# Hybrid encoder trunk on one core: one weight split moved from POOL to VectorE, and four squares and three head-pair splits moved to POOL

## The chip, the cores and the metric

The kernel runs on one core of a Trainium2 chip. The metric is the time of one execution on the device in microseconds (us). Several executions of the kernel before gave a median of 967.95 us. The engines are called as the profile calls them: PE is TensorE (its matmuls; PEld its weight loads), DVE is VectorE, ACT is ScalarE, POOL is GpSimd, SP issues the DMAs, and PSUM is the memory into which PE writes its results.

## The reference

The input is 512 frames of 1024 channels in fp32. Two layers follow each other; each is a mixer and a feed-forward block, both with an RMS norm ahead and a residual sum behind. The first layer's mixer pools over trailing windows, the second's is chunked attention with 16 heads of 64 channels. The change lies in and just ahead of the attention, which is this:

```python
qkv = h @ w_qkv                              # h: the normed input
q, k, v = jnp.split(qkv, 3, axis=-1)
q = head_rmsnorm(q.reshape(B, S, N_HEADS, HEAD_DIM), q_norm)
k = head_rmsnorm(k.reshape(B, S, N_HEADS, HEAD_DIM), k_norm)
...
s = jnp.einsum('bqhd,bkhd->bhqk', qc, kb).astype(jnp.float32) * scale + bias[None]
s = jnp.where(valid[None, None, None, :], s, -1e30)
p = jax.nn.softmax(s, axis=-1).astype(vb.dtype)
return jnp.einsum('bhqk,bkhd->bqhd', p, vb)  # then joined and multiplied by w_o
```

`head_rmsnorm` divides each head's 64 numbers by the root of their mean square: these are the squares that the change speaks of.

## The kernel before

**Split products.** Every fp32 product is made from parts. A matrix is split into a rounded part `hi` and the rest `lo` (`split`, L97 to L103: `hi` is a copy, on ACT unless another engine is named; `lo` is a subtraction, on DVE unless another is named), and PE makes three products, hi·hi, hi·lo and lo·hi, which it sums in PSUM (`mm3`, L121). Weights come by DMA and are split once they land (`load_split`, L110).

**Stages.** The first layer fills the span up to about 335 us. From there `opening` (a list of steps written by hand, with the order of PE, DVE, ACT and SP as written) makes the values, the norm's statistics and the first projection. The attention loop runs from about 440 us, and the second feed-forward block closes the program.

**The attention loop.** Work is a list of 64 tiles, 16 heads by four blocks of 128 frames. At each tile PE gets, in this order: `scores` of that tile (L1394 and L1395; DVE adds the bias and takes the minimum at L1398, ACT makes the exponentials at L1400 and scales by the reciprocal sums at L1402, all in tiles `sb`), at two places in each head pair `channel_major` (four transposes `zt` at L1364 that bring a projected pair into channel order, then ACT and DVE at L107, L108, L1368 and L1371 split it and POOL copies a half at L1375), `turn` of the tile two places back (transposes `tp` at L1410 of the scaled tile `sb`, split at L102 and L103 into `pt0` or `pt1`), and `mix` of the head whose last tile is four places back (`oo` at L1422; ACT copies half of it into `ob` at L1427 and DVE adds it into the pair's output `o` at L1428). Between these steps `fill` pulls matmuls from a list of fillers in proportion to the loop's progress: `second` (the second projection, begun in `opening`), `project(2)`, `project(3)` and then the output products `wo`.

**A projection.** `project(c)` makes queries and keys of heads 4c to 4c+3, that is of two head pairs. `products` (L1279) takes four slices of the weights `wqk`, each with two column halves: the matmuls `qk` at L123 to L125. `hi` of a slice is made by ACT, `lo` by POOL, since `project` hands `nc.gpsimd` as `eng` (L1314). For the second projection the first slice is `ready`: `opening` has loaded and split it (L1261 and L1262, `lo` on DVE). When a frame block t is done, `evict(t)` copies it into `Z[c, t]` (the tiles `z`; even t by ACT at L1310, odd t by DVE at L1308), and `squares(t)` is put off to the next step of the loop: ACT squares it into `zs` (L1300), DVE sums each head's 64 squares (L1301). Behind the four of them comes `norms` (L1315): two small operations on DVE (`qk_a`), a logarithm and an exponential on ACT (L135, L136, `qk_t` and `qk_y`), four more on DVE (L137 to L139, L1319), and then four multiplications of the tiles `z` by `qk_y` on POOL (L1321). The transposes `zt` of the pair need those four tiles.

**Splits of head pairs.** When the last head of a pair is mixed, the pair's output `O2[kept]` is split for the output products into `XS[kept]` and `XS[KD + kept]` (L1482): two halves of the tiles that the profile calls `two`, `hi` by ACT and `lo` by DVE. The weights `wo` of the output products for pairs one to six are split by POOL (`wo_h` at L100, `wo_l` at L103).

**What sets the order.** In the attention loop PE's order is that of the code. The orders of ACT, DVE, POOL and SP are set by the scheduler of the framework, from its own estimates of when each operation can run, and are then fixed in the program: each engine runs its list from front to back and waits at an operation whose input isn't there.

Of the kernel before, what the change touches and what calls it, by code (L numbers as in the profile page):

```python
# [19 lines left out]
AF = mybir.ActivationFunctionType  # L20
# [6 lines left out]
KD = D // P  # L27
# [45 lines left out]
def trunk(ctx: ExitStack, tc: tile.TileContext, xt, xT, cols, band, edge, poolw, gv, wout, wqk, wv, wo, rel, out):  # L73
    nc = tc.nc
# [14 lines left out]
    def psum(tag, name, bufs=2):  # L89
        return ps.tile([P, S], F32, name=name, tag=tag, bufs=bufs)  # L90
# [3 lines left out]
    def g_tile(name):  # L94
        return tmp.tile([P, S], F32, name=name, tag="g", bufs=6)

    def split(raw, hi, lo, eng=None, eng_hi=None):  # L97

        if eng_hi:
            eng_hi.tensor_copy(hi, raw)  # L100
        else:
            nc.scalar.activation(hi, raw, AF.Copy)  # L102
        return (eng or nc.vector).tensor_sub(lo, raw, hi.bitcast(F32))  # L103
# [6 lines left out]
    def load_split(src, n, name, pool=None, eng=None, tag=(None, None), eng_hi=None):  # L110

        raw = wp.tile([P, 1024], F32, name=f"{name}_r", tag="wr")
        if pool:
            hi, lo = (pool.tile([P, n], F32R, name=f"{name}_{c}", tag=t, bufs=2 if t == "as" else 1) for c, t in zip("hl", tag))
        else:
            hi, lo = (wp.tile([P, 1024], F32R, name=f"{name}_{c}", tag=f"w{c}", bufs=2) for c in "hl")
        nc.sync.dma_start(raw[:, :n] if len(src.shape) == 2 else raw.rearrange("p (a b) -> p a b", a=src.shape[1]), src)
        split(raw[:, :n], hi[:, :n], lo[:, :n], eng, eng_hi)
        return hi, lo

    def mm3(o, sh, sl, mh, ml, first, last, **how):  # L121

        yield nc.tensor.matmul(o, sh, mh, start=first, stop=False, **how)  # L123
        yield nc.tensor.matmul(o, sh, ml, start=False, stop=False, **how)  # L124
        yield nc.tensor.matmul(o, sl, mh, start=False, stop=last, **how)  # L125

    def run(steps):
        step = None
        for step in steps:
            pass  # L130
        return step

    def rsqrt(a, y, t):

        nc.scalar.activation(t, a, AF.Ln)  # L135
        seed = nc.scalar.activation(y, t, AF.Exp, scale=-0.5)  # L136
        nc.vector.scalar_tensor_tensor(t, y, -0.5, y, op0=OP.mult, op1=OP.mult)  # L137
        nc.vector.tensor_mul(t, t, a)
        return seed, nc.vector.scalar_tensor_tensor(y, t, 1.5, y, op0=OP.add, op1=OP.mult)  # L139
# [775 lines left out]
    def attention(rest, hook, hidden_slots):  # L915
        XS = set2
        O2, V, Z, QK, SM = {}, {}, {}, {}, {}
# [6 lines left out]
        def norms_of(c):  # L924
            return [big.tile([P, 8 * TT], F32, name=f"qk{c}_{v}", tag="nw", bufs=4) for v in "sayt"]

        def by_frame(v):
            return v.rearrange("p (t h) -> p t h", t=TT)
# [350 lines left out]
        def products(ov, w, name, eng=None, evict=None, ready=None):  # L1279

            for kk in range(4):
                hi, lo = ready if ready and kk == 0 else load_split(w[kk], 1024, f"{name}_{kk}", eng=eng)

                for c, t in [(c, t) for c in range(2) for t in range(TT)] if kk < 3 else [(c, t) for t in range(TT) for c in range(2)]:
                    k = 2 * kk + c
                    s = slice(c * S, (c + 1) * S)
                    q = slice(t * P, (t + 1) * P)
                    yield from mm3(ov[t], XS[k][:, q], XS[KD + k][:, q], hi[:, s], lo[:, s], k == 0, k == KD - 1)
                    if kk == 3 and c and evict:
                        evict(t)  # L1290

        def project(c, banks="PQ", ready=None):

            ov = [psum(banks[t // 2], f"qk{c}_{t}", BANKS[banks]) for t in range(TT)]
            ss, a, y, t_ = norms_of(c)
            s3, a3, y3 = (by_frame(v) for v in (ss, a, y))

            def squares(t):
                sq = g_tile(f"zs{c}_{t}")
                nc.scalar.activation(sq, Z[c, t].rearrange("p h d -> p (h d)"), AF.Square)  # L1300
                nc.vector.tensor_reduce(s3[:, t, :], sq.rearrange("p (h d) -> p h d", d=HD), axis=mybir.AxisListType.X, op=OP.add)  # L1301


            def evict(t):
                Z[c, t] = z = zp.tile([P, 8, HD], F32, name=f"z{c}_{t}", tag="z", bufs=8)
                flat = z.rearrange("p h d -> p (h d)")
                if t % 2:
                    nc.vector.tensor_copy(flat, ov[t])  # L1308
                else:
                    nc.scalar.activation(flat, ov[t], AF.Copy)  # L1310
                late.append(lambda: squares(t))

            yield from products(ov, wqk[c], f"wqk{c}", nc.gpsimd, evict, ready)

            def norms():  # L1315
                nc.vector.tensor_mul(a3, s3, r2[:, :, None].to_broadcast([P, TT, 8]))
                nc.vector.tensor_scalar(a, a, EPS, None, op0=OP.add)
                rsqrt(a, y, t_)
                nc.vector.tensor_mul(y3, y3, rcol[:, :, None].to_broadcast([P, TT, 8]))  # L1319
                for t in range(TT):  # L1320
                    nc.gpsimd.tensor_mul(Z[c, t], Z[c, t], y3[:, t, :, None].to_broadcast([P, 8, HD]))  # L1321

            late.append(norms)
# [34 lines left out]
        def channel_major(p, i):  # L1358


            zt = psum("S", f"zt{p}_{i}", 4)
            for t in range(TT):
                j = 4 * i + 2 * (p % 2)
                nc.tensor.transpose(zt[:, t * P:(t + 1) * P], Z[p // 2, t][:, j:j + 2, :].rearrange("p h d -> p (h d)"), ident)  # L1364
            zh, z2 = (big.tile([P, S], F32R, name=f"z{c}{p}_{i}", tag="zqk", bufs=8) for c in "h2")
            zl = None if i else g_tile(f"zl{p}_{i}")
            if i:
                nc.scalar.activation(zh, zt, AF.Copy, scale=gq[:, i:i + 1])  # L1368
                for e in range(2):
                    hs = slice(e * HD, (e + 1) * HD)  # L1370
                    nc.vector.scalar_tensor_tensor(KL[p % 2][e][hs], zt[hs], gq[hs, i:i + 1], zh[hs].bitcast(F32), op0=OP.mult, op1=OP.subtract)  # L1371
            else:
                split_scaled(zt, gq[:, i:i + 1], zh, zl)

            nc.gpsimd.tensor_copy(z2[HD:], zh[HD:].bitcast(F32))  # L1375
            moves = [(z2[:HD], (z2 if i else zl)[HD:]), (zh[HD:], (zh if i else zl)[:HD])]
            for o, x in moves:
                nc.sync.dma_start(o.bitcast(F32), x if x.dtype == F32 else x.bitcast(F32))
            QK[p, i] = (zh, z2)
# [65 lines left out]
        with tc.manual_schedule(engines={mybir.EngineType.PE}):  # L1445
            cur, done, kept = 0, 0, 0

            def fill(upto):

                nonlocal cur, done  # L1450
                while cur < len(fillers):
                    g, n, a, b = fillers[cur]
                    due = n * (upto - a) / (b - a)
                    while done < min(due, n):
                        next(g)
                        done += 1
                    if upto < b:
                        return
                    run(g)
                    cur, done = cur + 1, 0  # L1460

            fill(0)
            for i in range(nb + LAG + LAGM):
                steps = []
                if i < nb:
                    steps.append(lambda: scores(*tiles_[i]))
                if i % 8 in CM and i // 8 + 1 < NPAIR:
                    steps.append(lambda: channel_major(i // 8 + 1, CM.index(i % 8)))
                j = i - LAG
                if 0 <= j < nb:  # L1470
                    steps.append(lambda: turn(*tiles_[j]))
                j2 = j - LAGM
                if 0 <= j2 < nb and j2 % TT == TT - 1:
                    steps.append(lambda: mix(tiles_[j2][0]))
                for x, step in enumerate(steps):
                    step()
                    if late and x < 2:
                        late.pop(0)()
                    fill(i + (x + 1) / len(steps))

                while 8 * kept + 7 <= j2 and (cur == 3 or cur == 2 and done >= 24 * (kept // 2 + 1)):
                    split(O2[kept], XS[kept], XS[KD + kept])  # L1482
                    kept += 1
            fill(nb + FO)
        assert kept == NPAIR
# [96 lines left out]
```

## Time and profile before

| what | value |
|---|---|
| median of 3 runs | 967.95 us (967.49 to 968.1) |
| the profiled execution | 968.78 us |
| its span, from the first to the last instruction | 967.0 us |
| mean granted clock of TensorE | 1.00 |
| PE busy | 956.6 us (99%), 4958 matmuls |
| DVE busy | 848.4 us (88%) |
| ACT busy | 593.9 us (61%) |
| POOL busy | 94.5 us (10%), 82 instructions |
| DMA, mean over the span | 107 GB/s |

A row of the timeline has the start of an instruction counted from the span's start, its length, its engine, the line of the kernel, the operation, what it writes and reads (numbers left out of the names), the shape, and, where the engine stood idle ahead of it, how long and for whom. Consecutive instructions of a kind can be shown as one row with their count; the length then runs from the first one's start to the last one's end. Matmuls are pipelined: in a full stretch one of 512 columns starts some 0.23 us behind the other, though each is shown as 0.39 or 0.40 us long, so that a stall of PE is read from the distance of starts. The windows view gives the busy time of each engine in a stretch, with the number of instructions.

### The profile page before, as it was taken

What the parts mean: (1) busy time and instruction counts of PE and PEld (TensorE: products, weight loads), DVE (VectorE), ACT (ScalarE), POOL (GpSimd) and SP (SyncE); (2) the same over time, 40 slices, a digit from 0 to 9 for tenths busy, and PEclk for the clock granted to TensorE, in tenths of its full rate; (3) what the DMA queues carried; (4) which work ended last, traced back from release to release, by engine and by line L of the source; (5) the groups of instructions that cost most, each with busy time, mean ns of one, the idle gap of its engine ahead of it and who ended that gap; (6) DMA issues with size and microseconds to landing.
All of it is one profiled execution on the core that took longest, in us unless ns stands there. A gap on an engine that the chain in (4) does not pass through costs nothing.

```text
span 967.0 us, 13737 instructions
## 1 busy us (share of the span) xinstructions
PE 956.6 (99%) x4958; PEld 810.7 (84%) x4958; DVE 848.4 (88%) x1521; ACT 593.9 (61%) x1023; POOL 94.5 (10%) x82
## 2 busy tenths in 40 slices
PE   8999999999999999999999999999999999999998
PEld 7788988888888888888888787888988888888886
DVE  8999999999899859895777887999999999989953
ACT  7665554655555447466898888656565565466531
POOL 2300000000000000044435442000000000000000
PEclk9999999999999999999999999999999999999999
DMA  8222332332323317024443241332233233332323
GB/s 344 70 99 71 115 107 82 120 119 80 113 82 120 101 46 294 22 66 130 126 122 97 87 119 55 100 110 80 93 115 107 84 121 113 100 104 79 115 77 112
DMA packets 38996, 103.87 MB, mean 107 GB/s; under 512 B 4464, under 2 KB 7936, under 8 KB 38928
## 3 DMA queue, kind: packets, MB, share of 16 engines
q1 hardware_dynamic: 38864, 102.95, 32.8%
q8 instruction: 39, 0.64, 0.3%
q14 instruction: 29, 0.24, 0.1%
q0 software_dynamic: 32, 0.04, 0.0%
q10 hardware_dynamic: 32, 0.00, 0.0%
HBM read 96.65 MB, written 2.14 MB: 102 GB/s over the span
## 4 chain that ended last, share of the span: by engine, by line
PE 87%; DVE 9%; ACT 2%; DMA 1%; issue 1%; DVEq 0%; ACTq 0%
PE st_m L593 10%; PE out L124 8%; PE out L125 8%; PE out L123 8%; PE st_m L595 5%; PE st_t L593 5%; PE gv L124 4%; PE gv L123 4%; PE gv L125 4%; PE qk L123 3%; PE qk L124 3%; PE qk L125 3%; PE st_t L595 3%; PE st_b L593 3%; PE tp L1410 2%; DVE one L108 1%
## 5 line engine op out<-in xcount | busy, mean ns | idle before, releaser
L124 PE MATMUL out<-one,ow_h 128*128 128x512 f32 x224 | 88.2, 394 | 0.0
L123 PE MATMUL out<-one,ow_h 128*128 128x512 f32 x224 | 88.0, 393 | 0.0
L125 PE MATMUL out<-one,ow_l 128*128 128x512 f32 x224 | 88.0, 393 | 0.0
L829 DVE TENSOR_TENSOR X<-out,X 128x512 f32<-128x512 f32 (+1 forms) x65 | 44.4, 685 | 46.0 <-PE out L125 45.7
L593 PE MATMUL st_m<-two,g_h 128*128 128x512 f32 x240 | 75.2, 394 | 0.4 <-ACT v L602 0.4
L593 PE MATMUL st_m<-h,g_h 128*128 128x512 f32 x240 | 74.1, 390 | 0.0
L392 ACT ACTIVATE ow_h<-wo_r 128x768 fp32r<-128x768 f32 (+1 forms) x56 | 44.5, 794 | 42.9 <-PE out L124 40.7
L407 DVE SCALAR_TENSOR_TENSOR c<-a,col,c 128x511 f32<-128x511 f32 (+1 forms) x76 | 57.0, 752 | 0.0
L593 PEld LDWEIGHTS st_m<-h,g_h 128*128 128x128 f32 x240 | 45.1, 188 | 10.3
L595 PEld LDWEIGHTS st_m<-two,g_l 128*128 128x128 f32 x240 | 45.1, 188 | 9.6
L593 PEld LDWEIGHTS st_m<-two,g_h 128*128 128x128 f32 x240 | 44.0, 188 | 10.8 <-ACT w L602 0.8
L393 DVE TENSOR_TENSOR ow_l<-wo_r,ow_h 128x768 fp32r<-128x768 f32 (+1 forms) x56 | 50.5, 902 | 2.2 <-ACT ow_h L392 2.2
L602 ACT ACTIVATE w<-st_m 128x512 f32<-128x512 f32 x30 | 18.0, 599 | 56.0 <-PE st_m L595 56.0
L595 PE MATMUL st_m<-h,g_l 128*128 128x256 f32 x240 | 48.3, 283 | 0.0
L595 PE MATMUL st_m<-two,g_l 128*128 128x256 f32 x240 | 47.6, 280 | 0.0
L1398 DVE CUSTOM_DVE_ANT_0 sb<-sc,B 128x128 f32<-128x128 f32 (+1 forms) x64 | 31.1, 486 | 18.3 <-PE sc L1395 14.0
L124 PEld LDWEIGHTS out<-one,ow_h 128*128 128x128 f32 x224 | 42.4, 189 | 5.6 <-DVE one L418 0.3
L125 PEld LDWEIGHTS out<-one,ow_l 128*128 128x128 f32 x224 | 42.4, 189 | 5.5
L123 PEld LDWEIGHTS out<-one,ow_h 128*128 128x128 f32 x224 | 42.4, 189 | 5.4
L404 ACT ACTIVATE c<-a,col 128x512 f32<-128x512 f32 x38 | 30.7, 813 | 23.5 <-DVE a L751 21.8
L1400 ACT ACTIVATE sb<-sb,mx 128x128 f32<-128x128 f32 (+1 forms) x64 | 35.7, 558 | 10.5 <-DVE mx L1398 9.9
L392 ACT ACTIVATE g_h<-sa 128x1024 fp32r<-128x1024 f32 x32 | 33.8, 1057 | 12.0 <-DVE sa L638 7.3
(458 smaller groups left out, 3041.7 us busy)
## 6 DMA issues: line engine op xcount, KB each, us to landing
gv_r<-gv SPq DMA_DIRECT2D x86, 512.0 KB, 3.8
wo_r<-wout SPq DMA_DIRECT2D x32, 384.0 KB, 3.1
wo_r<-wout SPq DMA_DIRECT2D x32, 320.0 KB, 2.9
wqk_r<-wqk SPq DMA_DIRECT2D x12, 512.0 KB, 3.4
b<-wv SPq DMA_DIRECT2D x8, 512.0 KB, 6.6
wo_r<-wo SPq DMA_DIRECT2D x8, 512.0 KB, 3.5
xt<-xt SPq DMA_DIRECT2D x4, 512.0 KB, 5.2
X<-xT SPq DMA_DIRECT2D x8, 256.0 KB, 7.5
```

Of the source, the lines that this page charges most:

```text
L123: yield nc.tensor.matmul(o, sh, mh, start=first, stop=False, **how)
L124: yield nc.tensor.matmul(o, sh, ml, start=False, stop=False, **how)
L125: yield nc.tensor.matmul(o, sl, mh, start=False, stop=last, **how)
L392: nc.scalar.activation(hi[:, :n], raw[:, :n], AF.Copy)
L393: return hi, lo, lambda: nc.vector.tensor_sub(lo[:, :n], raw[:, :n], hi[:, :n].bitcast(F32))
L404: nc.scalar.activation(c, a, AF.Identity, scale=cw[2], bias=cw[3])
L407: nc.vector.scalar_tensor_tensor(c[:, j:], a[:, :S - j], cw[2 - j], c[:, j:], op0=OP.mult, op1=OP.add)
L593: nc.tensor.matmul(o, hi[:, c], B[i, name], start=first and i == 0, stop=False, **how)
L595: nc.tensor.matmul(o[:, 0], lo[:, c], B[i, name][:, 0], start=False, stop=i == 3, **how)
L829: nc.vector.tensor_add(X[d][:, fs], o[:, fs], X[d][:, fs])
L1398: nc.vector.tensor_tensor_reduce(out=s_[:, :n], in0=sc[:, :n], in1=BT[h % 2][:, :n][:, ::-1], scale=1.0, scalar=3e38, op0=OP.add, op1=OP.m ...
L1400: nc.scalar.activation(s_[:, :n], s_[:, :n], AF.Exp, scale=-1.0, bias=mx[:, 0:1], accum_out=mx[:, 1:2])
```

## The change

There are three edits, and they have nothing to do with each other in the code:

```diff
         def products(ov, w, name, eng=None, evict=None, ready=None):
...
-                hi, lo = ready if ready and kk == 0 else load_split(w[kk], 1024, f"{name}_{kk}", eng=eng)
+                hi, lo = ready if ready and kk == 0 else load_split(w[kk], 1024, f"{name}_{kk}", eng=None if ready and kk == 1 else eng)
...
             def squares(t):
                 sq = g_tile(f"zs{c}_{t}")
-                nc.scalar.activation(sq, Z[c, t].rearrange("p h d -> p (h d)"), AF.Square)
+                if c == 3:
+                    nc.gpsimd.tensor_mul(sq, Z[c, t].rearrange("p h d -> p (h d)"), Z[c, t].rearrange("p h d -> p (h d)"))
+                else:
+                    nc.scalar.activation(sq, Z[c, t].rearrange("p h d -> p (h d)"), AF.Square)
...
                 while 8 * kept + 7 <= j2 and (cur == 3 or cur == 2 and done >= 24 * (kept // 2 + 1)):
-                    split(O2[kept], XS[kept], XS[KD + kept])
+                    eng = nc.gpsimd if 2 < kept < 6 else None
+                    split(O2[kept], XS[kept], XS[KD + kept], eng, eng)
                     kept += 1
```

Part one: only the second projection is given `ready`, so the second slice of its weights (`kk == 1`) has its `lo` made by DVE and not by POOL. Part two: the four squares of the fourth projection (`c == 3`, heads 12 to 15) are multiplications on POOL and no longer ACT's. Part three: of head pairs four to six (`kept` 3, 4 and 5) POOL makes the copy `hi` and the subtraction `lo`, which ACT and DVE made. Lines behind L1300 move down by three, and by four behind L1482.

PE's order is the same in both programs. POOL's list grows by ten instructions, ACT's loses seven, DVE's loses two, and the scheduler has given all three some other orders. The first place is DVE's list at the end of `opening`, where `one` are tiles of the normed input, `c` is the last copy out of PSUM and `wqk_1_l` is the weight part of part one:

```order
 L108 SCALAR_TENSOR_TENSOR one_90<-y_4140,n_y,one_90 128x2x64 x2
 L108 SCALAR_TENSOR_TENSOR one_91<-y_4140,n_y,one_91 128x2x64 x2
+L103 TENSOR_TENSOR wqk_1_l<-wqk_1_r,wqk_1_h 128x1024
 L1268 COPY c_4222<-va_3706 128x512
 L108 SCALAR_TENSOR_TENSOR one_94<-y_4141,n_y,one_94 128x2x64 x2
```

The subtraction stands between the four operations on `one` and the copy of `c`. POOL loses it from its list.

The second place is ACT's list where the fourth projection's norm falls among the tiles of heads 9 and 10 (`sb_0` to `sb_3` are the tiles of one head, L1400 its exponentials and L1402 the scaling; `tp_0` and `tp_1` the first transposes of head 9). Before:

```order
L1402 ACTIVATE sb_0_5518<-sb_0_5518,mx_0_5519 128x128
L102 ACTIVATE pt1h<-tp_0_5581 128x128
L135 ACTIVATE qk_t<-qk_a 128x32
L136 ACTIVATE qk_y<-qk_t 128x32
L1400 ACTIVATE sb_2_5573,mx_2_5574<-sb_2_5573,mx_2_5574 128x384
L1402 ACTIVATE sb_1_5552<-sb_1_5552,mx_1_5553 128x256
L1400 ACTIVATE sb_3_5590,mx_3_5591<-sb_3_5590,mx_3_5591 128x512
L1402 ACTIVATE sb_2_5573<-sb_2_5573,mx_2_5574 128x384
L102 ACTIVATE pt1h<-tp_1_5598 128x2x128
L1402 ACTIVATE sb_3_5590<-sb_3_5590,mx_3_5591 128x512
L1427 ACTIVATE ob_5614<-oo_5604 64x512
```

And in the changed kernel:

```order
L1405 ACTIVATE sb_0_5518<-sb_0_5518,mx_0_5519 128x128
L102 ACTIVATE pt1h<-tp_0_5581 128x128
L1403 ACTIVATE sb_2_5573,mx_2_5574<-sb_2_5573,mx_2_5574 128x384
L1405 ACTIVATE sb_1_5552<-sb_1_5552,mx_1_5553 128x256
L1405 ACTIVATE sb_2_5573<-sb_2_5573,mx_2_5574 128x384
L1403 ACTIVATE sb_3_5590,mx_3_5591<-sb_3_5590,mx_3_5591 128x512
L102 ACTIVATE pt1h<-tp_1_5598 128x2x128
L1405 ACTIVATE sb_3_5590<-sb_3_5590,mx_3_5591 128x512
L1430 ACTIVATE ob_5614<-oo_5604 64x512
L135 ACTIVATE qk_t<-qk_a 128x32
L1403 ACTIVATE sb_0_5623,mx_0_5624<-sb_0_5623,mx_0_5624 128x128
L136 ACTIVATE qk_y<-qk_t 128x32
```

The norm's logarithm and exponential have gone from ahead of head 9's third exponential to behind `ob`, with head 10's first exponential between them.

The third place is DVE's list in the same stretch (`zs_3` is the last of the four squares, `o_3` the output of head pair four, `o_4` that of pair five, the ISA rows are the bias sums of L1398, two rows for each). Before:

```order
L1428 TENSOR_TENSOR o_3_5352<-oo_5498,ob_5507 64x512
L1301 TENSOR_REDUCE qk_s<-zs_3_5524 128x8
L1398 ISA sb_1_5552,mx_1_5553<-sc_1_5549,B_4307 128x256
L1398 ISA mx_1_5553 128x1
L103 TENSOR_TENSOR pt0l<-tp_2_5529,pt0h 128x3x128
L1401 RECIPROCAL mx_0_5519<-mx_0_5519 128x1
L1316 TENSOR_TENSOR qk_a<-qk_s,r_3421 128x32
L103 TENSOR_TENSOR two_101<-o_3_5352,two_97 128x512
L103 TENSOR_TENSOR pt0l<-tp_3_5560,pt0h 128x4x128
L1317 TENSOR_SCALAR qk_a<-qk_a 128x32
L1398 ISA sb_2_5573,mx_2_5574<-sc_2_5570,B_4307 128x384
```

And in the changed kernel:

```order
L1401 ISA sb_3_5590,mx_3_5591<-sc_3_5587,B_4307 128x512
L1401 ISA mx_3_5591 128x1
L1304 TENSOR_REDUCE qk_s<-zs_3_5524 128x8
L1404 RECIPROCAL mx_3_5591<-mx_3_5591 128x1
L103 TENSOR_TENSOR pt1l<-tp_1_5598,pt1h 128x2x128
L1319 TENSOR_TENSOR qk_a<-qk_s,r_3421 128x32
L1320 TENSOR_SCALAR qk_a<-qk_a 128x32
L1401 ISA sb_0_5623,mx_0_5624<-sc_0_5620,B_4306 128x128
L1401 ISA mx_0_5624 128x1
L1431 TENSOR_TENSOR o_4_5605<-oo_5604,ob_5614 64x512
L1404 RECIPROCAL mx_0_5624<-mx_0_5624 128x1
L137 SCALAR_TENSOR_TENSOR qk_t<-qk_y 128x32
```

The sum over the last squares has gone from behind `o_3` to behind head 9's fourth bias sum; L138, L139 and L1322 follow L137 at once. On POOL the squares, copies and subtractions stand between the old operations: `zs_0` ahead of the first `wo_l`, `zs_3` and the copy of `o_3` ahead of the second `wo_l`, the subtraction of `o_3` behind it and ahead of the four multiplications of L1321.

## Prediction before the result

> **What bounds the kernel now.** The first view is the page's line of busy times, the second the windows of the stretch that the change touches, with busy time and, in brackets, instructions of PE, PEld, DVE, ACT and POOL, then the granted clock, the DMA share and GB/s.
>
> ```profile
> PE 956.6 (99%) x4958; PEld 810.7 (84%) x4958; DVE 848.4 (88%) x1521; ACT 593.9 (61%) x1023; POOL 94.5 (10%) x82
> 430.00:460.00 30.00, 29.70 (x135) 24.29 (x134) 18.61 (x44) 18.63 (x45) 10.88 (x7) 1.00 0.40 122
> 460.00:530.00 70.00, 70.00 (x389) 59.09 (x388) 53.24 (x160) 62.87 (x152) 30.25 (x23) 1.00 0.41 116
> 530.00:600.00 70.00, 67.57 (x384) 55.80 (x383) 57.15 (x174) 61.85 (x159) 28.13 (x22) 1.00 0.32 93
> 600.00:700.00 100.00, 99.46 (x517) 85.28 (x516) 94.86 (x149) 58.15 (x86) 0.00 (x0) 1.00 0.28 93
> ```
>
> PE is the bound. Outside these windows an edit to another engine gains nothing, and inside them PE is idle for 0.30, 0.00, 2.43 and 0.54 us: a ceiling of 3.3 us on any gain, or a little more, since the shown length of a matmul covers some of each stall. The third view is what PE waits for from 425 to 620 us, in total, times, longest:
>
> ```profile
> PE tp L1410 <- ACT sb L1402: 1.6, 4, 0.8
> PE sc L1394 <- DMA zh<-zh: 0.7, 1, 0.7
> PE oo L1422 <- DVE pt1l L103: 0.5, 1, 0.5
> PE qk L123 <- DVE c L1268: 0.3, 1, 0.3
> ```
>
> The transposes `tp` that wait for ACT are the largest, the copy `c` is the place of part one. What a stall is worth stands in the starts:
>
> ```profile
> 546.70 0.40 PE L125 MATMUL wo<-two,wo_l 128*128 128x512 f32 x1
> 546.93 0.40 PE L123 MATMUL wo<-two,wo_h 128*128 128x512 f32 x1
> 548.15 0.44 PE L1410 MATMUL tp<-ident,sb 128*128 128x128 f32 x2 [0.82 <-ACT sb L1402]
> 586.26 0.40 PE L123 MATMUL wo<-two,wo_h 128*128 128x512 f32 x1
> 586.85 0.33 PE L1410 MATMUL tp<-ident,sb 128*128 128x128 f32 x1 [0.19 <-ACT sb L1402]
> ```
>
> Undisturbed, the next matmul starts 0.23 us behind (546.70 to 546.93). From 546.93 to 548.15 it is 1.22, so 0.99 are lost; from 586.26 to 586.85 it is 0.59, so 0.36.
>
> **Part one: the subtraction of `wqk_1_l`.**
>
> ```profile
> 435.38 1.23 DVE L1262 TENSOR_TENSOR wqk_l<-wqk_r,wqk_h 128x1024 fp32r<-128x1024 f32 x1
> 436.36 2.50 POOL L103 TENSOR_TENSOR wqk_l<-wqk_r,wqk_h 128x1024 fp32r<-128x1024 f32 x1 [12.19 <-ACT wqk_h L102]
> 436.51 3.29 DVE L108 SCALAR_TENSOR_TENSOR one<-y,n_y,one 128x128 fp32r<-128x128 f32 x4
> 439.72 0.68 DVE L1268 COPY c<-va 128x512 f32<-128x512 f32 x1
> 439.76 0.39 PE L125 MATMUL qk<-wqk_h,two 128*128 128x512 f32 x1
> 440.32 0.86 DVE L108 SCALAR_TENSOR_TENSOR one<-y,n_y,one 128x128 fp32r<-128x128 f32 x3
> 440.45 0.50 PE L123 MATMUL qk<-wqk_h,two 128*128 128x512 f32 x1 [0.30 <-DVE c L1268]
> ```
>
> Three operations on `one` with POOL idle take 0.86 us, 0.29 each; four beside POOL's subtraction take 3.29, and they end 0.94 behind POOL (439.80 against 438.86). Four undisturbed would be 1.15. So this DVE form stands still while POOL reads. [...]
>
> In the changed kernel DVE runs the four in 1.15 (436.51 to 437.66), the subtraction in 1.23 (to 438.89; its `hi` is an ACT copy that POOL's start at 436.36 shows done) and `c` in 0.68, to 439.57, where it ended at 440.40. PE wants the PSUM buffer 0.23 behind 439.76, at 439.99. The stall, 0.69 less 0.23 or 0.46, goes, and so does the slow first matmul behind it (0.50 for 0.39): **0.57 us gained**. PE is full behind it until 530 us (70.00 of 70.00), so that nothing takes this back there.
>
> **Part two: squares on POOL, and what it does to the norm.** POOL's price is the row of the same shape in L1321; the other rows are the norm's way.
>
> ```profile
> L1321 POOL TENSOR_TENSOR z<-z,qk_y 128x512 f32<-128x512 f32 x12 | 12.6, 1080 | 14.6 <-DVE qk_y L1319 14.6
> 541.76 0.63 ACT L1300 ACTIVATE zs<-z 128x512 f32<-128x512 f32 x1
> 543.42 0.69 DVE L1301 TENSOR_REDUCE qk_s<-zs 128x8 f32<-128x512 f32 x1
> 546.52 0.23 ACT L135 ACTIVATE qk_t<-qk_a 128x32 f32<-128x32 f32 x1 [0.27 <-DVE qk_a L1317]
> 546.99 0.62 ACT L1400 ACTIVATE sb<-sb,mx 128x384 f32<-128x384 f32 x1
> 547.61 0.49 ACT L1402 ACTIVATE sb<-sb,mx 128x256 f32<-128x256 f32 x1
> 547.23 0.69 DVE L1398 CUSTOM_DVE_ANT_0 sb<-sc,B 128x512 f32<-128x512 f32 x1
> 548.37 0.19 DVE L1319 TENSOR_TENSOR qk_y<-qk_y,n_y 128x32 f32<-128x32 f32 x1
> 548.64 4.05 POOL L1321 TENSOR_TENSOR z<-z,qk_y 128x512 f32<-128x512 f32 x4 [5.15 <-DVE qk_y L1319]
> 550.93 0.40 ACT L1400 ACTIVATE sb<-sb,mx 128x128 f32<-128x128 f32 x1
> 553.85 0.60 PE L1364 MATMUL zt<-ident,z 128*128 128x128 f32 x4
> ```
>
> ACT loses four squares of 0.63, some 2.5 us. That is worth what ACT's waits give back. Ahead of 546.99 ACT stood idle for 0.27 and then ran the logarithm and the exponential, all for the norm: 0.74 us from 546.25 to 546.99, between the split of `tp_0` and the work for `tp_1`. In the new order they stand behind `ob`. So the scaling that `tp_1` waits for (547.61 to 548.10) comes 0.74 earlier, and with the slack of the squares some 0.2 more, about 547.15. PE would be ready at 546.93 + 0.23 = 547.16. **The stall of 0.99 nearly goes: 0.9 gained.** The stall of `tp_0` ahead of it keeps its exponential in front, and I give it 0.1. Ends for the two together: 0, if another operation of ACT moves up into the gap, and 1.1.
>
> The same move makes the norm late. The sum over the last squares stood at 543.42; now it stands behind head 9's fourth bias sum (547.23, ending at about 547.6 with PE's gain and loss in it). It ends near 548.2, `qk_a` follows behind a split of `tp_1` at 549.4, ACT reaches the logarithm behind `ob` at 549.75, then head 10's first exponential (0.40 and its accumulator) and the norm's exponential to 550.6, and DVE's four small operations at some 0.23 each end at 551.5. Before, the last of them ended at 548.56: 2.95 later. POOL's four multiplications take 4.05 and would end at 555.65, where they ended at 552.69. PE's four transposes `zt` stood at 553.85 to about 554.15 and had 1.2 to 1.5 us to spare; with the 0.97 gained they would be wanted at 552.9 to 553.2. The last can't start before 555.65: **a new stall of about 2.5 us**. Its ends: 1.3, if the chain finds 1.2 us (the norm's exponential need not wait for the whole of head 10's), and 3.5, if one more operation of 0.7 to 1.1 us gets ahead of it. I take 2.5, since each step is an order that is fixed and a length from a row.
>
> **Part three: pair splits on POOL.**
>
> ```profile
> L100 POOL CAST wo_h<-wo_r 128x1024 fp32r<-128x1024 f32 x6 | 6.2, 1040 | 20.8 <-issue 7.8 <-PE wo L124 6.9 <-PE qk L125 6.1
> 541.08 2.42 POOL L103 TENSOR_TENSOR wo_l<-wo_r,wo_h 128x1024 fp32r<-128x1024 f32 x1
> 542.69 0.69 DVE L1428 TENSOR_TENSOR o<-oo,ob 64x512 f32<-64x512 f32 x1
> 543.67 0.61 ACT L102 ACTIVATE two<-o 128x512 fp32r<-128x512 f32 x1
> 550.63 0.39 PE L124 MATMUL wo<-two,wo_h 128*128 128x512 f32 x1
> ```
>
> Half a row of 1.04 for the copy and half of 2.42 for the subtraction: about 0.5 and 1.2 us a pair on POOL. `o_3` is there at 543.38; the copy ends at 543.9, the second `wo_l` at 546.3 and the subtraction at 547.6, or 548.2 if POOL falls behind with the squares. PE first reads it at 550.63, 549.7 with the gain: 1.5 us to spare, so no cost. If that cover were gone, each tenth that POOL is late would be a tenth of PE. The two later pairs fall where POOL is idle longer. What ACT saves (0.6 a pair) is spare except at head 14, whose first scaling now stands ahead of the second exponential, and the stall at 586.26 can go: **0.3 gained** of 0.36, ends 0 and 0.5. On the queue of SP two loads and two moves change places; the wait for the move `zh` (0.7) stays as long, because POOL's copies behind its multiplications and PE are late alike: 0, ends 0.3 on either side.
>
> **The sum**, against the profiled execution's own 968.78 us (span 967.0, so 1.8 around it): −0.57 − 0.1 − 0.9 + 2.5 − 0.3 + 0, or about +0.6, which gives 969.4 for a profiled one. It lies 0.8 above the median of the runs; the same difference on the median gives **968.5 us**. What a measurement of this kernel can tell from no change is 0.2%, 1.94 us, so 966.0 and 969.9 are the bounds. What is gained at `tp_0` and `tp_1` is lost again at `zt`, whatever its size: up to there the sum is only the chain's end against the transposes of before, 555.65 against 554.15, or +1.5. With the chain's ends that is 0.3 to 2.5, so that this case reaches from −0.57 + 0.3 − 0.5, or 967.2 us, to −0.57 + 2.5 + 0.3, or 970.2.
>
> **The rivals.** *The norm is in time.* If the multiplications are done when PE asks, what is left is −0.57 − 0.1 − 0.9 − 0.3, −1.9: 966.05 us, on the bound of faster. For it speaks that the squares and the sums have time enough (POOL can make the last square by 542.2); against it, the place of the sum and of the logarithm in the two lists, each of which would have to be read wrongly. It needs qk_y by 549 us. Chance 0.17, half of it below 966.0.
>
> *POOL stops DVE.* The squares `zs_2` and `zs_3` would run at 538 to 542, where DVE makes `zl` and `kl`:
>
> ```profile
> 540.30 1.50 DVE L1371 SCALAR_TENSOR_TENSOR kl<-zt,gq,zh 64x512 fp32r<-64x512 f32 x2
> 541.43 0.40 PE L123 MATMUL wo<-two,wo_h 128*128 128x512 f32 x1
> 541.95 0.52 PE L1410 MATMUL tp<-ident,sb 128*128 128x128 f32 x3
> ```
>
> PE's transposes at 541.95 came 0.15 behind the end of `kl`, with 0.29 lost. If each of the two squares (1.08) held DVE as POOL's subtraction held it at 436.51, `kl` would end 2.2 later and PE with it: +0.6 + 2.2, or 970.7, slower. It decides from 1.4 us on. Against it: `kl` and `o` read one operand from PSUM, and `o` at 542.69 took 0.69 wholly beside POOL's 2.42 (541.08 to 543.50). Chance 0.12. [...]
>
> *Only part one counts.* ACT's gap at `tp_1` fills up and the norm comes in time by its old slack: −0.57, 967.4 us. Nothing in the lists supports both. Chance 0.11.
>
> **How the numbers follow.** The forecast has 0.60, its own range 967.2 to 970.2. Below 966.0 lies half of the first rival, 0.09, and a little for gains that no row shows: 0.11 faster. Above 969.9 lie the second rival and the tail of the forecast, where the norm's chain is later still: 0.15 slower. The rest, 0.74, is within 0.2%. The range from 966.0 to 970.0 leaves out the lower half of the first rival and the second.
>
> **What the profile after would show.** Right: `c` ends near 439.6 and PE has no wait there; PE's starts around `tp_1` are 0.3 us apart or less; the multiplications of L1324 start near 551.5 and PE waits for them at `zt` for 2 to 3 us; DVE's rows beside POOL's squares keep their 0.7 us. The forecast is wrong if `zt` waits for less than 1 us (then the first rival), if DVE's rows of L1374 are longer than 1.5 us for the two (the second), or if `tp_1` waits as before.

## The result, and the profile after

The changed kernel took 969.55 us (median of 15 runs, 968.45 to 970.64), the kernel before 967.71 (15 runs, 967.24 to 971.49). The ratio of the two is 1.0018, with a 95% interval from 1.0011 to 1.0025: the change costs 1.1 to 2.4 us. The profiled execution of the changed kernel took 970.64 us with a span of 968.8; it is the longest of the 15.

These are, of the kernel after, the windows from 430 to 460 and from 530 to 600 us, and what PE waits for from 425 to 620 us:

```profile
430.00:460.00 30.00, 30.00 (x139) 24.88 (x138) 18.32 (x47) 19.08 (x46) 7.95 (x5) 1.00 0.39 123
530.00:600.00 70.00, 67.47 (x372) 55.53 (x370) 54.92 (x169) 56.32 (x147) 36.75 (x32) 0.98 0.33 93
```

```profile
PE zt L1367 <- POOL z L1324: 1.9, 3, 0.7
PE tp L1413 <- ACT sb L1405: 0.8, 3, 0.4
PE oo L1425 <- DVE pt1l L103: 0.5, 1, 0.5
```

The wait for `c` is gone, and 430 to 460 us is full. ACT gave up 5.5 us in the second window (61.85 to 56.32) and POOL took 8.6 (28.13 to 36.75); over the whole program POOL runs 91 instructions against 82, since ten come and one goes. PE's waits for `tp` fell from 1.6 us to 0.8, and a new wait for POOL's multiplications stands on top with 1.9. And the granted clock, 1.00 before, is 0.98. Part one and the two ends of the new wait, as rows of the timeline:

```profile
436.95 1.13 DVE L108 SCALAR_TENSOR_TENSOR one<-y,n_y,one 128x128 fp32r<-128x128 f32 x4
438.00 1.22 DVE L103 TENSOR_TENSOR wqk_l<-wqk_r,wqk_h 128x1024 fp32r<-128x1024 f32 x1
439.13 0.69 DVE L1268 COPY c<-va 128x512 f32<-128x512 f32 x1
440.34 0.39 PE L123 MATMUL qk<-wqk_h,two 128*128 128x512 f32 x1
551.36 4.05 POOL L1324 TENSOR_TENSOR z<-z,qk_y 128x512 f32<-128x512 f32 x4 [3.42 <-DVE qk_y L1322]
552.60 0.27 PE L1367 MATMUL zt<-ident,z 128*128 128x128 f32 x1
553.46 0.33 PE L1367 MATMUL zt<-ident,z 128*128 128x128 f32 x1 [0.59 <-POOL z L1324]
555.47 0.33 PE L1367 MATMUL zt<-ident,z 128*128 128x128 f32 x1 [0.67 <-POOL z L1324]
```

The four operations on `one` take 1.13 where they took 3.29 beside POOL's subtraction. At `zt` the four transposes, 0.11 apart before, start within 2.87 us (552.60 to 555.47): the last three each wait for their multiplication. The last view is the granted clock by the microsecond in and behind that wait (the third number from the end of a row):

```profile
554.00:555.00 1.00, 0.33 (x1) 0.14 (x1) 1.00 (x3) 0.20 (x1) 1.00 (x2) 1.00 0.00 0
555.00:556.00 1.00, 0.53 (x3) 0.50 (x4) 0.16 (x2) 0.88 (x3) 1.00 (x2) 1.00 0.00 0
556.00:557.00 1.00, 1.00 (x6) 0.76 (x5) 0.45 (x1) 1.00 (x3) 0.75 (x2) 0.79 0.00 0
557.00:558.00 1.00, 1.00 (x4) 0.71 (x4) 0.90 (x2) 0.19 (x1) 0.92 (x2) 0.50 0.00 0
559.00:560.00 1.00, 1.00 (x5) 0.90 (x4) 0.59 (x1) 0.83 (x3) 0.94 (x2) 0.51 0.41 93
560.00:562.00 2.00, 2.00 (x13) 1.82 (x13) 1.60 (x5) 1.31 (x4) 0.37 (x1) 1.00 0.76 184
```

PE has come back to full work by 556 us, and from about 556.6 to 560 it is granted half its clock (0.50).

Since PE's order is the same in both programs, the start of each matmul can be set against that of the same matmul before. The table gives these differences in us, counted from the last matmul ahead of the stall at `c` (the executions differ by up to 0.6 us before that place, which says nothing of the change). The two columns on the right are second profiles, of the experiments below.

| at the matmul that started before at | after | after, second profile | before, second profile |
|---|---|---|---|
| 456.7, behind part one | −0.63 | −0.63 | +0.05 |
| 553.6, ahead of `zt` | −1.60 | −1.55 | 0.00 |
| 554.2, the last `zt` | +0.94 | +0.96 | −0.01 |
| 558.5, where the clock was low | +2.60 | +1.03 | −0.01 |
| 568.2, behind the wait for the move `zh` | +1.70 | +0.09 | −0.94 |
| 962.8, the end | +1.53 | −0.08 | −0.99 |

So part one gives 0.63, the ACT waits at `tp` 0.97 (0.92 in the second profile), `zt` takes 2.54 (2.51), the stretch behind it 1.66 more in the execution with the low clock (0.50) and 0.07 in the other (1.00), and behind that up to 0.2 comes back. The step at 568.2 is no gain of the change: the second profile of the kernel before has it too.

Beside POOL's squares these operations of DVE ran as long as they do without them (`kl` took 1.50 before as well, and the sums of L1301 0.68 or 0.69):

```profile
538.01 1.04 POOL L1301 TENSOR_TENSOR zs<-z 128x512 f32<-128x512 f32 x1
538.58 0.67 DVE L1304 TENSOR_REDUCE qk_s<-zs 128x8 f32<-128x512 f32 x1
540.79 1.04 POOL L1301 TENSOR_TENSOR zs<-z 128x512 f32<-128x512 f32 x1
539.96 1.50 DVE L1374 SCALAR_TENSOR_TENSOR kl<-zt,gq,zh 64x512 fp32r<-64x512 f32 x2
```

### The profile page after: what moved, and what is told of

It reads as the page before. It is cut to its first block, busy times and chain, and to the rows that moved or that the text cites. A ratio compares the mean times of both kernels' runs of the same rounds, so it can differ in the third digit from the quotient of the medians.

```text
span 968.8 us, 13746 instructions
## 1 busy us (share of the span) xinstructions
PE 958.8 (99%) x4958; PEld 812.9 (84%) x4958; DVE 846.2 (87%) x1519; ACT 590.4 (61%) x1016; POOL 100.7 (10%) x91
```

## The experiments

**Theory and rivals.** Theory A: time is PE's path alone; what the change gains at `c` and `tp` it loses at `zt`, because the squares on POOL move the norm's steps to late places in the lists. Rival B: the price is POOL's added work beside DVE.

**Part one alone.**

```diff
-... load_split(w[kk], 1024, f"{name}_{kk}", eng=eng)
+... load_split(w[kk], 1024, f"{name}_{kk}", eng=None if ready and kk == 1 else eng)
```

> Part one alone. Theory of PE's path (A): the stall at the copy c and the slow matmul behind it go, 0.57 to 0.65 us, and nothing takes it back: 0.6 us below the kernel before, ratio 0.9994; the wait of PE for c is gone from the list of waits. Rival (B, the cost of the whole change comes from more work on POOL beside DVE): the same here, since POOL loses work. Only a longer stretch of DVE's operations on one than 1.15 us would speak against both.

Measured: ratio 0.9994 (0.9985 to 1.0003), 967.17 us. PE's starts show the same 0.63 us at the same place, and nothing takes it back. The interval alone would not settle it; the starts do.

**Parts one and three**, the kernel before with part one's line and:

```diff
-                    split(O2[kept], XS[kept], XS[KD + kept])
+                    eng = nc.gpsimd if 2 < kept < 6 else None
+                    split(O2[kept], XS[kept], XS[KD + kept], eng, eng)
```

> Parts one and three without the squares. A: the norm of the fourth projection stays early in the lists, so PE does not wait at zt and the granted clock stays 1.00; part one gives 0.6, one copy less on ACT ahead of tp_1 about 0.5, head 14 up to 0.3: 1.0 to 1.4 us below the kernel before, ratio 0.9985 to 0.9990. B: three copies and three subtractions more on POOL (1.7 us a pair) cost DVE time, so at or above the kernel before, ratio 1.000 to 1.002.

Measured: ratio 1.0001 (0.9992 to 1.0010), 968.74 us (the medians, 968.74 and 967.96 for the kernel before beside it, differ by 0.8), so A as stated fell. The profiled execution is the longest of the eleven (970.27 us), and three of the eleven show a mean clock of 0.998. PE does not wait at `zt`, but these rows of POOL, DVE, ACT and PE stand in its timeline:

```profile
543.45 2.39 POOL L103 TENSOR_TENSOR wo_l<-wo_r,wo_h 128x1024 fp32r<-128x1024 f32 x1
545.80 1.29 POOL L103 TENSOR_TENSOR two<-o,two 128x512 fp32r<-128x512 f32 x1
544.38 1.51 DVE L1316 TENSOR_TENSOR qk_a<-qk_s,r 128x32 f32<-128x32 f32 x1
546.41 0.71 DVE L1317 TENSOR_SCALAR qk_a<-qk_a 128x32 f32<-128x32 f32 x1
547.16 0.23 ACT L135 ACTIVATE qk_t<-qk_a 128x32 f32<-128x32 f32 x1 [2.26 <-DVE qk_a L1317]
546.28 0.40 PE L123 MATMUL wo<-two,wo_h 128*128 128x512 f32 x1
548.79 0.44 PE L1410 MATMUL tp<-ident,sb 128*128 128x128 f32 x2 [2.11 <-ACT sb L1402]
```

The small product `qk_a` took 1.51 us and ended with POOL's subtraction `wo_l` (543.45 and 2.39, so 545.84); undisturbed the same operation takes 0.18, as in the kernel after:

```profile
548.80 0.18 DVE L1319 TENSOR_TENSOR qk_a<-qk_s,r 128x32 f32<-128x32 f32 x1
```

The next one, 0.71, ended at 547.12 as POOL's subtraction for pair four was ending (547.09). ACT's logarithm stood ahead of its other work and waited 2.26, and PE lost 2.28 at `tp` (546.28 to 548.79, less 0.23), 1.3 more than before. Behind it the clock was low again (0.55 and 0.50 in the second and third row):

```profile
547.00:548.00 1.00, 0.00 (x0) 0.00 (x0) 0.97 (x6) 0.84 (x4) 0.09 (x1) 1.00 0.00 0
549.00:550.00 1.00, 1.00 (x5) 0.81 (x4) 0.35 (x2) 1.00 (x3) 0.72 (x1) 0.55 0.00 0
551.00:552.00 1.00, 1.00 (x5) 0.94 (x4) 0.00 (x0) 0.11 (x2) 1.00 (x2) 0.50 0.76 124
553.00:554.00 1.00, 1.00 (x8) 0.84 (x7) 0.99 (x5) 0.64 (x3) 0.32 (x1) 1.00 0.73 257
```

So what B names does happen where the norm's two small operations of DVE, whose inputs lie in SBUF, fall on POOL's subtractions: they took 1.51 and 0.71 us, and in the kernel after 0.18 each. It does not hold for all that DVE reads from SBUF: the sum at 538.58, shown above, took 0.67 beside POOL's square and was not held up. In the whole change the norm's steps come when POOL is idle (its row at 551.36 has 3.42 us of idle time ahead of it), so that this is not its price.

**Part two alone.**

```diff
-                nc.scalar.activation(sq, Z[c, t].rearrange("p h d -> p (h d)"), AF.Square)
+                if c == 3:
+                    nc.gpsimd.tensor_mul(sq, Z[c, t]..., Z[c, t]...)
+                else:
+                    nc.scalar.activation(sq, Z[c, t].rearrange("p h d -> p (h d)"), AF.Square)
```

> Part two alone: the squares on POOL, the lists put the last steps of the norm behind the fourth split of head 9, later than in the whole change. A: the multiplications start 2 to 3 us later than in the whole change, PE waits at zt for about 5 us in all and the granted clock falls behind it for some 3.4 us, which costs 1.6 more: 4 to 6 us above the kernel before, ratio 1.004 to 1.006. B: only half of the added POOL work of the whole change is here, so at most what the whole change costs, +1 us, ratio 1.001 or less.

Measured: ratio 1.0079 (1.0066 to 1.0091), 975.73 us: further than A said, and eight times what B allows for half of POOL's work. POOL's multiplications started at 555.03, where the whole change has 551.36, since the lists put the norm's last step behind the fourth split of head 9; PE's wait is this:

```profile
PE zt L1367 <- POOL z L1324: 4.4, 4, 2.9
PE tp L1413 <- ACT sb L1405: 2.1, 4, 1.1
```

By PE's starts `zt` took 5.7, the low clock behind it 1.6, and a `tp` that waits for ACT 1.2 more, which I had not foreseen. The low clock (0.50) lasted 6.8 us here (555.74 to 562.57) and began within the wait. So the parts do not add up: part one alone gives some 0.6 us, parts one and three together cost at most 0.8, part two alone costs some 7.7, and all three cost 1.8, since each program gets lists of its own.

**The whole change, with the multiplications in quarters.**

```diff
-                for t in range(TT):
-                    nc.gpsimd.tensor_mul(Z[c, t], Z[c, t], y3[:, t, :, None].to_broadcast([P, 8, HD]))
+                for j, m in ((0, 2), (4, 2), (2, 2), (6, 2)) if c == 3 else ((0, 8),):
+                    for t in range(TT):
+                        nc.gpsimd.tensor_mul(Z[c, t][:, j:j + m], Z[c, t][:, j:j + m], y3[:, t, j:j + m, None].to_broadcast([P, m, HD]))
```

> The whole change, with each of the four multiplications of the fourth projection's norm cut in four, in the order in which the transposes ask for them: the parts for the first transposes are done after 4 of 16 pieces, about 1.2 us behind qk_y. A: PE hardly waits at zt (under 0.3 us), the clock stays at 1.00, and the gains stay: 1.5 to 2.2 us below the kernel before, ratio 0.9978 to 0.9985. B: POOL has as much work as in the whole change and 12 more instructions, so as slow as that or slower, ratio 1.0015 to 1.003.

Measured: ratio 0.9999 (0.9990 to 1.0008), 967.66 us, 1.9 below the whole change; POOL worked longer for it (5.78 us for the 16 pieces against 4.05). B is out as the price of the whole. But the forecast for A was at least 1.2 us too good: 1.5 to 2.2 below the kernel before were forecast, and it is 0.3 below the 967.96 us of that kernel's runs beside it. The wait at `zt` is gone and the clock is 1.00, and these stand in its place:

```profile
PE tp L1414 <- DVE zl L108: 0.9, 1, 0.9
PE tp L1414 <- ACT sb L1406: 0.7, 3, 0.3
PE sc L1398 <- DVE pt1l L103: 0.6, 1, 0.6
```

From there to 558.5 PE loses 2.2 us again. The lists of ACT and DVE behind `zt` seem to run late against a PE that no longer waits; no experiment changed these lists alone. With the clock full the whole change loses hardly more over the same stretch (2.6 us in its second profile), so that by these profiles most of what the quarters gain over it is the clock.

**PE kept busy in the wait.** Whether the clock falls because PE stands idle:

```diff
+                for _ in range(4 if p == 6 and i == 0 and t else 0):
+                    nc.tensor.matmul(zt[:, t * P:(t + 1) * P], ident, ident, start=True, stop=True)
                 nc.tensor.transpose(zt[:, t * P:(t + 1) * P], ...)
```

> The whole change, and ahead of each of the second, third and fourth transposes of the late pair four small matmuls on a constant, which the transposes overwrite: PE still waits for POOL's multiplications, but with less idle time. Theory C (the granted clock falls because PE was idle in the wait): the multiplications end as before, the clock stays at 1.00 for more of the stretch and most of the 1.6 us go: 968.0 to 968.5 us, ratio 1.0003 to 1.0008. Rival D (the clock falls for another reason, or the loss is the wait alone): as the whole change or slower by the matmuls, ratio 1.0018 to 1.0025, clock 0.998.

Measured: ratio 1.0007 (0.9999 to 1.0016), 968.43 us, as theory C said. All eleven runs show a mean clock of 0.999 or 1.000, where nine of the whole change's 15 show 0.998, so that this isn't the chance of one execution. The multiplications hold PE's transposes as long as ever (+2.7 us by its starts), but the clock stays at 1.00:

```profile
553.00:554.00 1.00, 1.00 (x12) 1.00 (x11) 1.00 (x3) 0.25 (x1) 1.00 (x2) 1.00 0.00 0
557.00:558.00 1.00, 1.00 (x7) 0.85 (x7) 1.00 (x5) 1.00 (x3) 0.94 (x2) 1.00 0.00 0
```

**The multiplications in halves**, in place of the quarters:

```diff
-                for j, m in ((0, 2), (4, 2), (2, 2), (6, 2)) if c == 3 else ((0, 8),):
+                for j, m in ((0, 4), (4, 4)) if c == 3 else ((0, 8),):
```

> The whole change, with each of the four late multiplications cut in two: the halves that the first transposes need are done about 2.3 us behind qk_y (4 pieces, between the 0.36 us of a quarter and the 1.01 us of a whole one), so PE waits at zt for 0.5 to 1.0 us in place of 2.5. C: too short for the clock to fall, it stays 1.00; the stalls that the quarters showed behind zt come back in part, so 967.3 to 968.2 us, ratio 0.9995 to 1.0005. If so short a wait lowers the clock too, 969 us or more. D: ratio 1.0010 or more, since the loss would go with POOL's work.

Measured: ratio 1.0001 (0.9992 to 1.0010), 967.85 us. PE lost 0.8 us at `zt`, the clock stayed at 1.00, and 1.4 us were lost behind it at `zl` and `tp`, less than with the quarters. So a shorter wait is exchanged for later ones: with both, 2.2 us go between 553.6 and 558.5. One of the eleven runs shows a mean clock of 0.949 at 967.70 us, a time like the others', so that a mean clock alone doesn't measure a loss.

**Part one, and pairs five and six of part three.**

```diff
-                    split(O2[kept], XS[kept], XS[KD + kept])
+                    eng = nc.gpsimd if 3 < kept < 6 else None
+                    split(O2[kept], XS[kept], XS[KD + kept], eng, eng)
```

> Part one and, of part three, pairs five and six alone; pair four is split by ACT and DVE as before. Theory E (POOL's two-input operations hold up DVE operations that read only SBUF; pair four's subtraction and the second wo_l pushed behind its copy did it to qk_a): qk_a takes 0.2 us again, PE waits for tp_1 for 1.0 us as before and not 2.1, the clock stays 1.00: 0.6 to 0.8 us below the kernel before, ratio 0.9992 to 0.9994. Rival F (any split moved to POOL costs): ratio 1.0000 or above.

Measured: ratio 0.9995 (0.9986 to 1.0003), 967.15 us. The interval alone would not rule out F. But both operations on `qk_a` take 0.17 us again, and with pair four left to ACT and DVE the wait at `tp` is that of the kernel before (1.6 in all, 0.8 the longest), and PE's starts are as with part one alone up to `zh`, for which this execution waits 0.3. This is what tells pair four's split from the other two.

**Three squares**, added to the last experiment:

```diff
-                nc.scalar.activation(sq, Z[c, t].rearrange("p h d -> p (h d)"), AF.Square)
+                if c == 3 and t < 3:
+                    nc.gpsimd.tensor_mul(sq, Z[c, t]..., Z[c, t]...)
+                else:
+                    nc.scalar.activation(sq, Z[c, t].rearrange("p h d -> p (h d)"), AF.Square)
```

> Part one, pairs five and six of part three, and three of the four squares on POOL, the last one on ACT: the lists keep the sum of the last squares early and put the norm's logarithm and exponential just behind the scaling that tp_1 waits for. A and C and E together: the wait of tp_1 goes (0.9 us), qk_y comes at about 549 and PE waits at zt for 0.3 us at most, clock 1.00: 1.2 to 1.9 us below the kernel before, ratio 0.9980 to 0.9988. If POOL's squares cost by themselves, ratio 0.9994 or above.

Measured: ratio 0.9987 (0.9978 to 0.9996), 966.64 us, the best of all, and under both kernels. The number is in the forecast, the way isn't: PE's waits for `tp` are 1.6 in all as before, so that the number was met by luck. The stall has moved:

```profile
544.18 0.40 PE L125 MATMUL wo<-two,wo_l 128*128 128x512 f32 x1
545.40 0.33 PE L1413 MATMUL tp<-ident,sb 128*128 128x128 f32 x1 [0.83 <-ACT sb L1405]
547.35 0.44 PE L1413 MATMUL tp<-ident,sb 128*128 128x128 f32 x2 [0.22 <-ACT sb L1405]
```

`tp_1` waits for 0.22, but the sum over the third square now stands ahead of `o_3` and `tp_0` waits for 0.83. By PE's starts it gains what part one gives and no more, up to the place of `zh`; its lead over the last experiment is inside the intervals.

**The two kernels a second time**, without an edit.

> The kernel before, profiled a second time. If the wait of PE for the move zh (0.9 us of PE's starts near 565.6 us in the first profile) belongs to the kernel, it is there again. If it belonged to that one execution, it is gone or a good deal smaller, and the profiled time lies nearer to the median of 967.7 us than 968.78 did.

> The whole change, profiled a second time. The wait at zt is a matter of the lists and comes again with 2.5 us; what the lower clock costs behind it may differ, between 0 and 1.7 us, since the runs of the whole change lie between 968.5 and 970.6 us with mean clocks from 0.998 to 1.000. The wait for zh, gone in the first profile after, stays gone.

Measured: 967.32 us for the kernel before, 969.18 for the changed one. The first has no wait for `zh`:

```profile
PE tp L1410 <- ACT sb L1402: 1.5, 4, 0.8
PE oo L1422 <- DVE pt1l L103: 0.5, 1, 0.5
PE qk L123 <- DVE c L1268: 0.4, 1, 0.4
```

The move took 5.0 us to land, and 6.7 in the first profile: the 0.94 us belong to that execution and not to the kernel. In the changed kernel the wait at `zt` is the same (2.51 us), and the clock is not (1.00 where it was 0.50):

```profile
554.00:555.00 1.00, 0.33 (x1) 0.14 (x1) 0.95 (x2) 0.41 (x2) 1.00 (x2) 1.00 0.00 0
557.00:558.00 1.00, 1.00 (x8) 0.81 (x7) 1.00 (x2) 0.42 (x2) 0.92 (x2) 1.00 0.00 0
```

## Why the prediction was right, and where it was short

It forecast 968.5 us from 966.0 to 970.0; the result is 969.55, inside, and the change is a little slower, by 0.18% where 0.06% was forecast. By its steps:

- **Part one: right.** 0.57 was forecast and 0.63 measured, with the four operations at 1.13 (1.15), and nothing took it back.
- **ACT's waits at `tp`: right.** 1.0 forecast, 0.97 and 0.92 measured, and from the cause named: the norm's logarithm and exponential leave the gap.
- **The late norm: right.** The multiplications were to start near 551.5 and did at 551.36 (551.64 if the 0.35 us by which this execution lay behind at 440 us is taken off and part one's 0.63 is put back); the wait was to be 2.5 and is 2.54 and 2.51. The balance up to the last `zt`, +1.5 without part one, is +1.57 and +1.59.
- **Head 14: too large.** 0.3 was forecast; 0.4 us go at 586.26, but 0.3 come back at the next transposes, so 0.1 is left.
- **The wait for `zh`: mis-read.** It was taken as a part of the kernel that stays. It was one execution's: the second profile of the kernel before hasn't got it, and its 0.94 us are about the 0.8 between profile and median. The sum on the median is not hurt, as the wait dropped out of both.
- **What the sum left out: the clock.** The step "a new stall of about 2.5 us" was priced as 2.5. Behind it PE had half its clock (0.50) for 3.4 us in the first profile after, which cost 1.66 more, and its full clock in the second. With the clock full the balance against the second profile of before is +0.91 us (−0.08 + 0.99), near the forecast of +0.6; with the clock low it is +2.52 (1.53 + 0.99). The measured 1.1 to 2.4 lies between. Of the 15 runs nine show a mean clock of 0.998 and take 969.83 us on average, the six with 0.999 or 1.000 take 969.09. PE kept busy in the same wait brought the time to 968.43. So the clock is a part of what was missing, and its share is uncertain: keeping PE busy takes 1.1 us off by the ratios (1.0018 to 1.0007), but the six runs with the fuller clock lie only 0.74 below the other nine, and still 1.4 above the kernel before. What the rest is, no run shows.
- **The rival "POOL stops DVE": not here, but near.** Beside POOL's squares `kl` took 1.50 as before. Yet with the squares left on ACT two subtractions of POOL held up the two steps of `qk_a` (1.51 and 0.71), and in the profiled execution it cost 1.3 us more at `tp` and 1.5 in the low clock behind it. The prediction gave part three no cost because PE had 1.5 us to spare for pair four; it didn't ask what POOL's operations then fall upon. That it costs nothing in the whole change is owed to part two, which moves `qk_a` away.

What stays open: why the clock was 0.50 behind the wait in one profile after and 1.00 in the other was not shown, and a list in which the norm leaves ACT's gap and is still in time for `zt` was not found; with three squares on POOL the wait moved to `tp_0`.

## What to carry to other kernels

Where a scheduler writes the lists, read what a moved operation does to the places of its successors: four squares moved to an idle engine put a chain of small operations some 3 us later, and the wait for it, with the low clock that could follow, outweighed what the change gained. Behind stalls of PE of 2.1 and 2.5 us two profiles show a clock of 0.50, which cost up to 1.66 us more, and a third, with the stall of 2.5, shows 1.00: price such a stall with that beside its length. A wait seen in one profile is worth a second profile before a sum is built on it. Before work is given to an idle POOL, look at which operations of DVE will fall on it: here POOL's subtractions held up operations with two inputs in SBUF (the four on `one` took 3.29 us for 1.13, the product `qk_a` 1.51 for 0.18) and one `tensor_scalar` (0.71 for 0.18), while operations with one input from PSUM (`o` 0.69 beside a subtraction, `kl` 1.50 beside a square) and the sums (0.67 beside a square, 0.68 beside a subtraction in the run with three squares) were not held up.

## What the runs showed of the hardware

In the first profile after, PE was busy for 1.19 us of the three from 553 to 556, most of the wait at `zt`, and was granted 0.50 of its clock from 556.57 to 559.99 us. In the second profile it was busy for 1.09 of the same three microseconds, and the clock was 1.00 from 552 to 560. After 2.1 us of full idleness (parts one and three) the clock fell as well, to 0.55, 0.50, 0.50 and 0.74 in the four microseconds from 549 us, and in part two alone it was 0.50 for 6.8 us. With 0.8 us lost at `zt` (halves), and with small matmuls in the wait, it was 1.00. These are the 3.41 us ahead of the low clock in the first profile after, and the 3.41 us of it:

```profile
553.16:556.57 3.41, 1.76 (x8) 1.21 (x9) 1.64 (x7) 2.49 (x8) 3.23 (x4) 1.00 0.00 0
556.57:559.98 3.41, 3.41 (x13) 2.73 (x12) 2.21 (x5) 1.74 (x5) 3.20 (x3) 0.50 0.27 62
```

PE was not wholly idle ahead of the low clock: it was busy for 1.76 of the 3.41 us. The same wait had 1.66 us of loss behind it in one execution and 0.07 in the other; no run shows what tells the two apart.

Cutting POOL's multiplication in four made 16 pieces take 5.78 us where four took 4.05: a piece of 128x128 takes 0.36 us on average and one of 128x512 takes 1.01.
